# Last round of a mixture-of-experts tail: down weights by column halves, final scales spread by products, outputs on two queues

## The chip, the cores and the metric

One core of one Trainium2 chip runs the whole kernel in one launch. The metric is device time of one execution in microseconds (us), median of the runs shown.

## The reference, cut to what matters

Two transformer blocks over 256 rows of 1024 features, all in float32. The second block ends in a mixture of 32 experts and a last normalisation, and only this end is touched:

```
for e in range(32):
    hid = silu(xn @ w_gate[e]) * (xn @ w_up[e])          # 1024 -> 256
    out = out + (hid * cw[..., e:e+1]) @ w_down[e]       # 256 -> 1024, cw is 0 but for two experts a row
h = h + out
y = h * rsqrt(mean(h * h, axis=-1) + 1e-6) * final_norm_g      # 1024 scales, one a column
```

## The kernel before, in words

The experts are sorted by how many rows chose them, and only the chosen rows are gathered into places. Ten rounds follow (`NP` is 10). Rounds 0 to 3 take two experts with 64 places each, rounds 4 to 9 take four experts with 32 places each, so that 128 places fill the partitions in every round. A round `p` goes through these steps, each with a name in `moe`:

- `gu(p, 0)` and `gu(p, 1)` (line 1540) multiply the gathered rows by gate and up weights, half of the 1024 features at a time; `act(p)` (lines 1547 to 1549) makes the hidden values `hid`, 128 places by 256;
- `trans(p)` (line 1554) turns `hid` on TensorE, and ScalarE copies it out of PSUM as `hT` (line 1556);
- `dn(p)` (line 1562) multiplies `hT` by the down weights, 256 to 1024. The output is made in two halves of 512 columns, `c` 0 and 1; in each half two blocks of the 256 (`f` 0 and 1) are accumulated, and within each the experts follow one another. Each half is split into a rounded high part `y` on ScalarE (line 279) and the rest on VectorE (line 280);
- `scatter(p)` (line 1571) adds the places back to their rows: for each half of the columns and each half `t` of the rows, two products (high, then rest) into one of four accumulators `acc[t, c]` in PSUM.

The steps of neighbouring rounds are interleaved: `first(p)` holds `gu(p, 0)`; `down(p - 1)` holds `trans(p - 1)`, `scatter(p - 2)` for `c` 0, `dn(p - 1)`, and `scatter(p - 2)` for `c` 1; `second(p)` holds `gu(p, 1)` and `act(p)`. After the loop come `scatter(8)`, the load of the final scales, and `last`: `trans(9)`, `dn(9)` for both halves, `scatter(9)` for both halves. Then `write` normalises and sends out. This part of the kernel stands under a manual schedule: every engine, and every queue on which an engine issues transfers, runs its instructions in the order in which the program writes them.

Weights come through transfers that SyncE (SP) issues in the order of the list `self.raws`. A load (`Raw`) holds 1 MB, and there is room for 18 of them: 7 `big` and 3 `big2` buffers, and 16 small ones of which a load takes two. `_loads` hands out loads as long as a buffer is free, after each step. In round 9 the four experts' down weights take small buffers: each expert is fetched by two transfers of 512 KB, one for each `f`, with 4 KB of contiguous memory for each partition (line 1454). The final scales are one transfer from the same queue, whose source is repeated for all 128 partitions (line 1632).

`write` needs the sum of squares of each row. For each of the four accumulators ScalarE squares and sums (line 363); VectorE multiplies half 0 by its scales into `xgf` (line 1643), adds the two sums (line 1647), makes the mean (line 354), GpSimd raises it to the power -1/2 (line 356); then VectorE makes half 1 of the output (`o`, line 1652), ScalarE scales half 0 (line 1654), and SP issues four transfers of 256 KB to the output (lines 1653 and 1655).

Of the kernel before, what the change touches and what calls it, by code (L numbers as in the profile page):

```python
# [20 lines left out]
D = 1024  # L21
P = 128
# [77 lines left out]
class Net:  # L100
# [1317 lines left out]
    def moe(self):  # L1418
# [28 lines left out]
        def load_d(e):  # L1447
            def f(parts):
                rows = e.of(wd).rearrange("(p f) n -> p f n", f=2)
                if len(parts) == 1:  # L1450
                    nc.sync.dma_start(parts[0].rearrange("p (f c) n -> p f (c n)", f=2), rows)
                else:
                    for f in range(2):
                        nc.sync.dma_start(parts[f].rearrange("p c n -> p (c n)"), rows[:, f])
            return known(Raw(f, "d"), e)
        xs = self.xs
        def gu_of(raw, k):

            x = raw[k * len(raw) // 4].rearrange("p a b -> p (a b)").rearrange("p (j k n) -> p j k n", j=2, n=256)
            return x[:, :, k % (4 // len(raw)), :]  # L1460
        d_of = lambda raw, f, c: raw[0][:, 2 * f + c, :] if len(raw) == 1 else raw[f][:, c, :]
        oh, xg, stt, cwc, rsl = {}, {}, {}, {}, {}

        NP, NB = ROUNDS, BATCHES
# [92 lines left out]
        def dn(p, tiles, cols=range(2)):  # L1557
            for c in cols:
                q = self.pt()
                for f in range(2):  # L1560
                    for x, s in zip(tiles, own(p)):
                        nc.tensor.matmul(q[s], hT[p][:, f, s], d_of(x, f, c), start=f == 0, stop=f == 1)  # L1562
                h, l = self.act([P, 512], F32R, name="y"), self.act([P, 512], F32R, name="y")
                self.split(q, h, l)
                y[p, c] = (h, l)
# [13 lines left out]
                                     stop=False)  # L1579
        self.ids = None  # L1580
        gus = [[[load_gu(e, hf) for e in of_round(p)] for hf in range(2)] for p in range(NP)]
        ds = [[load_d(e) for e in of_round(p)] for p in range(NP)]
        for p in range(NP):
            if p:
                self.raws.extend(ds[p - 1])
            self.raws.extend(gus[p][0] + gus[p][1])
        self.raws.extend(ds[NP - 1])
        def first(p, tiles):
            gu(p, 0, tiles)
            b, j = divmod(p, 2)  # L1590
            if p == 0:
                gather(0, range(4, 8))
                slots_of(0)
                residual(1)
            if b < NB - 1 and j == 0:
                onehots(b + 1)
        def down(p, tiles):
            trans(p)
            if p:
                scatter(p - 1, [0])  # L1600
            dn(p, tiles)
            if p:
                scatter(p - 1, [1])
# [12 lines left out]
                self.rawpart(ds[p - 1], lambda *tiles, p=p: down(p - 1, tiles))  # L1616
            self.rawpart(gus[p][1], lambda *tiles, p=p: second(p, tiles))
        self.step(lambda: scatter(NP - 2))
        self.step(self.final_gain)
        def last(*tiles):  # L1620
            trans(NP - 1)
            for c in range(2):
                dn(NP - 1, tiles, [c])
            for c in range(2):
                scatter(NP - 1, [c])
        self.rawpart(ds[NP - 1], last)
        self.step(lambda: self.write([[acc[t, c] for c in range(2)] for t in range(2)]))

    def final_gain(self):

        self.gfin = self.act([P, D], name="gfin")
        self.nc.sync.dma_start(self.gfin, self.a["final_norm_g_2"][None, :].broadcast_to([P, D]))

    def write(self, x):

        nc, v, g = self.nc, self.nc.vector, self.gfin
        ss = [[self.small([P, 1]) for _ in range(2)] for _ in range(2)]
        xg = [self.act([P, 512], name="xgf") for _ in range(2)]
        for c in range(2):
            for t in range(2):  # L1640
                ss[t][c] = self.sumsq(x[t][c], 512)
                if c == 0:
                    v.tensor_tensor(xg[t], x[t][0], g[:, 0:512], op=ALU.mult)
        r = []
        for t in range(2):
            s = self.small([P, 1])
            v.tensor_tensor(s, ss[t][0], ss[t][1], op=ALU.add)
            r.append(self.power(s, D))
        for t in range(2):
            ts = slice(t * P, (t + 1) * P)  # L1650
            o = self.act([P, 512], name="o")
            v.scalar_tensor_tensor(o, x[t][1], r[t], g[:, 512:D], op0=ALU.mult, op1=ALU.mult)
            nc.sync.dma_start(self.out[0, ts, 512:D], o)
            nc.scalar.mul(xg[t], xg[t], r[t])
            nc.sync.dma_start(self.out[0, ts, 0:512], xg[t])

    def overflow(self):

# [2 lines left out]
        with self.tc.If(most >= 64 * 65):  # L1661
            left, m = self.act([P, 2 * E]), self.act([P, 2, 2, E])
            cap = self.act([P, E], name="cap")
            v.tensor_scalar(cap, self.key, self.order[:, WIDE - 1:WIDE], 32.0, op0=ALU.is_ge, op1=ALU.mult)
            v.tensor_scalar(cap, cap, 32.0 - 1000.0, None, op0=ALU.add)
            l3 = left.rearrange("p (t e) -> p t e", t=2)
            v.tensor_tensor(l3, self.pm, cap[:, None, :].to_broadcast([P, 2, E]), op=ALU.is_ge)
            v.tensor_tensor(m, self.sel2, self.w12[:, :, :, None].to_broadcast([P, 2, 2, E]), op=ALU.mult)
            for k in range(2):
                v.tensor_tensor(m[:, :, k, :], m[:, :, k, :], l3, op=ALU.mult)  # L1670
            v.tensor_tensor(l3, m[:, :, 0, :], m[:, :, 1, :], op=ALU.add)
            xT = [self.act([P, 4, S], name="xT") for _ in range(2)]
            for t in range(2):
                xn = self.act([P, D], name="xn")
                v.tensor_tensor(xn, *(x.bitcast(F32) for x in self.xs[t]), op=ALU.add)
                v.tensor_scalar(xn, xn, self.rf[:, t:t + 1], None, op0=ALU.mult)
                for i in range(2):
                    p = self.pt((P, 4, P))
                    for k in range(4):
                        kt = 4 * i + k  # L1680
                        nc.tensor.transpose(p[:, k, :], xn[:, kt * P:(kt + 1) * P], self.ident)
                        nc.scalar.mul(xT[i][:, k, t * P:(t + 1) * P], p[:, k, :], self.col("ffn_cols", kt, 1))
            self.X = [self.act([P, D], name="x") for _ in range(2)]
            for t in range(2):
                for c in range(2):
                    v.tensor_copy(self.X[t][:, c * 512:(c + 1) * 512], self.acc[t, c])
            for e in range(E):
                w = []
                for n in ("w_exp_gate_2", "w_exp_up_2"):
                    x = self.big([P, 8, 256], F32, "wo")  # L1690
                    for c in range(2):
                        rows = a[n][0, e, c * 512:(c + 1) * 512, :]
                        nc.sync.dma_start(x[:, 4 * c:4 * c + 4, :], rows.rearrange("(p k) n -> p k n", k=4))
                    w.append(x)
                wd = self.big([P, 2, D], F32, "wo")
                nc.sync.dma_start(wd, a["w_exp_down_2"][0, e].rearrange("(f p) n -> p f n", p=P))
                hid = self.act([P, 2, S], name="ho")
                for f in range(2):
                    q = []
                    for i in range(2):  # L1700
                        p = self.pt()[:, 0:S]
                        for k in range(8):
                            nc.tensor.matmul(p, w[i][:, k, f * P:(f + 1) * P], xT[k // 4][:, k % 4, :], start=k == 0,
                                             stop=k == 7)
                        q.append(p)
                    h = hid[:, f, :]
                    nc.scalar.activation(h, q[0], AF.Tanh, scale=0.5)
                    v.scalar_tensor_tensor(h, h, 1.0, q[0], op0=ALU.add, op1=ALU.mult)
                    v.tensor_tensor(h, h, q[1], op=ALU.mult)
                for t in range(2):  # L1710
                    for c in range(2):
                        p = self.pt()
                        for f in range(2):
                            nc.tensor.matmul(p, hid[:, f, t * P:(t + 1) * P], wd[:, f, c * 512:(c + 1) * 512],
                                             start=f == 0, stop=f == 1)
                        s = self.X[t][:, c * 512:(c + 1) * 512]
                        v.scalar_tensor_tensor(s, p, left[:, t * E + e:t * E + e + 1], s, op0=ALU.mult, op1=ALU.add)
            self.write([[x[:, 0:512], x[:, 512:D]] for x in self.X])


@with_exitstack
# [53 lines left out]
```

## Time and profile before

| what | value |
|---|---|
| median of 3 runs | 972.24 us (971.6 to 977.51) |
| profiled execution, its time | 971.25 us |
| profiled execution, its span | 969.5 us |
| busy share of the span: TensorE, VectorE, ScalarE, GpSimd | 93%, 56%, 49%, 4% |
| mean granted TensorE clock | 0.966 of full |

The span runs from the first to the last instruction of the program; the execution's own time is 1.75 us longer. The profiled execution lies 0.99 us under the median. In the rows below, PE is TensorE, PEld its weight loads, DVE is VectorE, ACT ScalarE, POOL GpSimd; SPq and ACTq are the queues on which SyncE and ScalarE issue transfers. Times are from the start of the span.

### The profile page before, as it was taken

Reading aid. Unit: us, or ns where it says so; the run is one execution under the profiler, and the core shown is the slowest. Engines: PE = TensorE matmul, PEld = TensorE weight load, DVE = VectorE, ACT = ScalarE, POOL = GpSimd, SP = SyncE. Lnnn points to the kernel's source line nnn. Section 1 sums busy time; section 2 is a strip of 40 time slices with the busy share of each in tenths; the row PEclk is TensorE's granted clock in tenths of the full one; section 3 lists DMA queues with packets and bytes.
Section 4 is the critical chain, followed back from the end, with each engine's and each line's share of the span. In section 5 each row is a group of like instructions: output and inputs, shape, how many; then the busy total and the mean of one; then the engine's idle time right before and its main releaser. Section 6 shows DMA issues by size and latency. Waiting matters only on the chain.

```text
span 969.5 us, 14260 instructions
## 1 busy us (share of the span) xinstructions
PE 900.0 (93%) x5265; PEld 697.7 (72%) x5265; DVE 547.4 (56%) x1101; ACT 472.6 (49%) x900; POOL 34.6 (4%) x71
## 2 busy tenths in 40 slices
PE   6999999999999999999999999999989999647775
PEld 5889898888999999988888887998864444213112
DVE  5986889776675555577765568755455221101002
ACT  5666789654664544456666635545432323002002
POOL 4200000000000000000200000000000000000000
PEclk9999999999999999999999999999998999779868
DMA  9644235495375555544854544454848999999994
GB/s 292 217 153 153 88 131 177 140 321 176 108 247 185 202 178 190 178 145 145 259 180 153 188 150 161 164 184 138 307 166 322 403 405 406 402 406 410 375 408 174
DMA packets 97784, 222.65 MB, mean 230 GB/s; under 512 B 9378, under 2 KB 13739, under 8 KB 96427
## 3 DMA queue, kind: packets, MB, share of 16 engines
q1 hardware_dynamic: 94016, 218.91, 63.5%
q10 hardware_dynamic: 3691, 2.74, 0.9%
q8 instruction: 44, 0.72, 0.3%
q14 instruction: 33, 0.27, 0.1%
HBM read 220.59 MB, written 1.05 MB: 229 GB/s over the span
## 4 chain that ended last, share of the span: by engine, by line
PE 80%; DMA 13%; DVE 3%; issue 1%; ACT 1%; POOL 0%; SPq 0%; DVEq 0%; ACTq 0%; POOLq 0%
PE acc L313 18%; PE acc L315 18%; PE acc L314 17%; DMA raw<-in_w_exp_up_dram 6%; PE pt L1540 5%; PE pt L314 3%; PE pt L315 3%; PE pt L313 3%; DMA rawa<-in_w_exp_down_dram 3%; PE pt L1562 2%; PE pt L1490 1%; DMA rawa<-in_w_exp_up_dram 1%; PE pt L286 1%; DMA raw<-in_w_exp_gate_dram 1%; PE acc L1571 1%
## 5 line engine op out<-in xcount | busy, mean ns | idle before, releaser
L280 DVE TENSOR_TENSOR w<-raw,w 128x512 fp32r<-128x512 f32 (+4 forms) x288 | 273.6, 969 | 115.6 <-ACT w L279 113.6
L279 ACT CAST w<-raw 128x512 fp32r<-128x512 f32 (+4 forms) x288 | 236.3, 847 | 153.9 <-PE acc L315 117.0
L313 PE MATMUL acc<-w,st 128*128 128x512 f32 (+2 forms) x508 | 197.2, 392 | 0.0
L314 PE MATMUL acc<-w,st 128*128 128x512 f32 (+2 forms) x508 | 196.9, 388 | 0.0
L315 PE MATMUL acc<-w,st 128*128 128x512 f32 (+2 forms) x508 | 192.9, 388 | 0.2 <-DVE w L280 0.2
L1540 PE MATMUL pt<-raw,xg 128*32 128x512 f32 (+1 forms) x360 | 95.7, 669 | 40.3 <-DMA raw<-in_w_exp_up_dram 40.3
L315 PEld LDWEIGHTS acc<-w,st 128*128 128x128 f32 x508 | 95.5, 188 | 18.9 <-DVE w L280 0.6
L313 PEld LDWEIGHTS acc<-w,st 128*128 128x128 f32 x508 | 95.8, 189 | 18.4 <-ACT st L279 0.5
L314 PEld LDWEIGHTS acc<-w,st 128*128 128x128 f32 x508 | 95.7, 189 | 17.4 <-DVE st L280 0.2
L1540 PEld LDWEIGHTS pt<-raw,xg 128*32 128x32 f32 (+1 forms) x360 | 22.1, 126 | 95.1 <-issue 91.4
L280 DVE TENSOR_TENSOR y<-pt,y 128x512 fp32r<-128x512 f32 x20 | 13.8, 692 | 129.3 <-ACT y L279 129.3
L314 PE MATMUL pt<-st,w 128*128 128x256 f32 x256 | 72.4, 283 | 1.9 <-DVE w L280 1.9
L315 PE MATMUL acc<-st,w 128*128 128x256 f32 x256 | 73.7, 288 | 0.0
L313 PE MATMUL acc<-st,w 128*128 128x256 f32 x256 | 73.5, 287 | 0.0
L314 PE MATMUL acc<-st,w 128*128 128x256 f32 x256 | 73.4, 287 | 0.0
L313 PE MATMUL pt<-st,w 128*128 128x256 f32 x256 | 72.3, 283 | 0.0
L315 PE MATMUL pt<-st,w 128*128 128x256 f32 x256 | 71.8, 283 | 0.0
L1556 ACT COPY hT<-pt 128x256 f32<-128x256 f32 x10 | 3.7, 373 | 97.4 <-PE pt L1554 97.4
L314 PEld LDWEIGHTS pt<-st,w 128*128 128x128 f32 x256 | 49.1, 192 | 2.3 <-DVE w L280 2.1
L313 PE MATMUL acc<-w,hid 128*128 128x512 f32 x128 | 50.0, 390 | 0.0
L314 PE MATMUL acc<-w,hid 128*128 128x512 f32 x128 | 49.9, 390 | 0.0
L315 PE MATMUL acc<-w,hid 128*128 128x512 f32 x128 | 49.8, 389 | 0.0
(393 smaller groups left out, 1391.0 us busy)
## 6 DMA issues: line engine op xcount, KB each, us to landing
raw<-in_w_in_dram SPq DMA_DIRECT2D x31, 1024.0 KB, 5.3
raw<-in_w_exp_gate_dram SPq DMA_DIRECT2D x45, 512.0 KB, 9.5
raw<-in_w_exp_up_dram SPq DMA_DIRECT2D x45, 512.0 KB, 10.2
rawa<-in_w_exp_down_dram SPq DMA_DIRECT2D x44, 512.0 KB, 9.1
raw<-in_w_up_dram SPq DMA_DIRECT2D x16, 1024.0 KB, 5.7
raw<-in_w_down_dram SPq DMA_DIRECT2D x16, 1024.0 KB, 6.2
raw<-in_w_exp_down_dram SPq DMA_DIRECT2D x10, 1024.0 KB, 11.0
rawa<-in_w_exp_gate_dram SPq DMA_DIRECT2D x38, 256.0 KB, 7.8
```

What stands on the lines that cost most here:

```text
L279: self.nc.scalar.copy(h, src)
L280: self.nc.vector.tensor_sub(l, src, h.bitcast(F32))
L286: self.nc.tensor.transpose(p[:, i, :], src[:, i * P:(i + 1) * P], self.ident)
L313: mm(acc, xh, wh, start=start, stop=False)
L314: mm(acc, xl, wh, start=False, stop=False)
L315: mm(acc, xh, wl, start=False, stop=stop)
L1490: nc.tensor.matmul(p, xs[t][i][:, k * P:(k + 1) * P], oh[b, t], start=n == 0, stop=n == 3)
L1540: nc.tensor.matmul(guP[p][q].rearrange("s (j f) -> s j f", j=2), xg[b, hf][:, k, j * P + q.start:j * P + q.stop], gu_of(x, k), start=kt == ...
L1556: nc.scalar.copy(hT[p], q)
L1562: nc.tensor.matmul(q[s], hT[p][:, f, s], d_of(x, f, c), start=f == 0, stop=f == 1)
L1571: nc.tensor.matmul(acc[t, c], stt[b][:, j, t, :], y[p, c][i], start=False, stop=p == NP - 1 and i == 1)
```

## The change

Three edits, all at the end.

1. The down weights of round 9 are loaded and used by halves of columns. A load now holds half `c` of the columns of two experts (`load_dc`), by two transfers of 512 KB, one for each expert; a partition's share of a transfer is two pieces of 2 KB. All of half 0 is asked for ahead of half 1. `last(c)` is called twice: for half 0 it does `trans(9)`, `final_gain`, `dn(9)` of half 0, `scatter(9)` of half 0, and the first part of `write`; for half 1 `dn`, `scatter`, and the rest of `write`.
2. The final scales come as one 4 KB transfer of 8 rows of 128, issued by ScalarE in `first(9)` (`load_gain`). `final_gain` spreads them to all partitions with eight products whose stationary operand is one column of the identity repeated 128 times, and two ScalarE copies out of PSUM.
3. `write` is cut in two: half 0's squares and scale products are written right behind half 0's `scatter`; the sum of both halves' squares is folded into the instruction that makes the mean. The two outputs `xgf` are issued by ScalarE instead of SP.

```diff
+        def load_dc(es, c):
+
+            def f(parts):
+                for i, e in enumerate(es):
+                    rows = e.of(wd).rearrange("(p f) n -> p f n", f=2)[:, :, c * 512:(c + 1) * 512]
+                    nc.sync.dma_start(parts[0][:, 2 * i:2 * i + 2, :] if len(parts) == 1 else parts[i], rows)
+            return known(Raw(f, "d"), es[1])
...
+        dc_of = lambda raw, i, f: raw[0][:, 2 * i + f, :] if len(raw) == 1 else raw[i][:, f, :]
...
                 for f in range(2):
-                    for x, s in zip(tiles, own(p)):
-                        nc.tensor.matmul(q[s], hT[p][:, f, s], d_of(x, f, c), start=f == 0, stop=f == 1)
+                    for i, s in enumerate(own(p)):
+                        w = d_of(tiles[i], f, c) if p < NP - 1 else dc_of(tiles[i // 2], i % 2, f)
+                        nc.tensor.matmul(q[s], hT[p][:, f, s], w, start=f == 0, stop=f == 1)
...
-        ds = [[load_d(e) for e in of_round(p)] for p in range(NP)]
+        ds = [[load_d(e) for e in of_round(p)] for p in range(NP - 1)]
+        tail = of_round(NP - 1)
+        ds_last = [[load_dc(tail[i:i + 2], c) for i in range(0, len(tail), 2)] for c in range(2)]
...
-        self.raws.extend(ds[NP - 1])
+        self.raws.extend(ds_last[0] + ds_last[1])
...
+            if p == NP - 1:
+                self.load_gain()
...
         self.step(lambda: scatter(NP - 2))
-        self.step(self.final_gain)
-        def last(*tiles):
-            trans(NP - 1)
-            for c in range(2):
-                dn(NP - 1, tiles, [c])
-            for c in range(2):
-                scatter(NP - 1, [c])
-        self.rawpart(ds[NP - 1], last)
-        self.step(lambda: self.write([[acc[t, c] for c in range(2)] for t in range(2)]))
+        def last(c, tiles):
+            if c == 0:
+                trans(NP - 1)
+                self.final_gain()
+            dn(NP - 1, tiles, [c])
+            scatter(NP - 1, [c])
+            self.write(c, [acc[t, c] for t in range(2)])
+        for c in range(2):
+            self.rawpart(ds_last[c], lambda *tiles, c=c: last(c, tiles))
+
+    def load_gain(self):
+
+        self.grow = self.act([P, P], name="grow")
+        self.nc.scalar.dma_start(self.grow[0:8, :], self.a["final_norm_g_2"].rearrange("(k n) -> k n", k=8))

     def final_gain(self):

         self.gfin = self.act([P, D], name="gfin")
-        self.nc.sync.dma_start(self.gfin, self.a["final_norm_g_2"][None, :].broadcast_to([P, D]))
-
-    def write(self, x):
+        for c in range(2):
+            p = self.pt((P, 4, P))
+            for i in range(4):
+                k = 4 * c + i
+                self.nc.tensor.matmul(p[:, i, :], self.ident[0:8, k:k + 1].to_broadcast([8, P]), self.grow[0:8, :],
+                                      start=True, stop=True)
+            self.nc.scalar.copy(self.gfin[:, c * 512:(c + 1) * 512], p.rearrange("q i n -> q (i n)"))
+
+    def write(self, c, x):

         nc, v, g = self.nc, self.nc.vector, self.gfin
...
+        if c == 0:
+            self.xgf, self.ms = [], []
             for t in range(2):
-                ss[t][c] = self.sumsq(x[t][c], 512)
-                if c == 0:
-                    v.tensor_tensor(xg[t], x[t][0], g[:, 0:512], op=ALU.mult)
+                ss = self.sumsq(x[t], 512)
+                xg, ms = self.act([P, 512], name="xgf"), self.small([P, 1])
+                v.tensor_tensor(xg, x[t], g[:, 0:512], op=ALU.mult)
+                v.tensor_scalar(ms, ss, 1.0 / D, EPS, op0=ALU.mult, op1=ALU.add)
+                self.xgf.append(xg)
+                self.ms.append(ms)
+            return
         r = []
         for t in range(2):
-            s = self.small([P, 1])
-            v.tensor_tensor(s, ss[t][0], ss[t][1], op=ALU.add)
-            r.append(self.power(s, D))
+            ss, ms, rt = self.sumsq(x[t], 512), self.small([P, 1]), self.small([P, 1])
+            v.tensor_scalar(ms, ss, 1.0 / D, self.ms[t], op0=ALU.mult, op1=ALU.add)
+            nc.gpsimd.tensor_tensor(rt, ms, self.mhalf[:, 0:1], op=ALU.pow)
+            r.append(rt)
         for t in range(2):
             ts = slice(t * P, (t + 1) * P)
             o = self.act([P, 512], name="o")
-            v.scalar_tensor_tensor(o, x[t][1], r[t], g[:, 512:D], op0=ALU.mult, op1=ALU.mult)
+            v.scalar_tensor_tensor(o, x[t], r[t], g[:, 512:D], op0=ALU.mult, op1=ALU.mult)
             nc.sync.dma_start(self.out[0, ts, 512:D], o)
-            nc.scalar.mul(xg[t], xg[t], r[t])
-            nc.sync.dma_start(self.out[0, ts, 0:512], xg[t])
+            nc.scalar.mul(self.xgf[t], self.xgf[t], r[t])
+            nc.scalar.dma_start(self.out[0, ts, 0:512], self.xgf[t])
```

## Rows read from the trace of the kernel before

**Rows 1.** The page: busy share of the 16 transfer engines in 40 equal slices.

```profile
DMA  9644235495375555544854544454848999999994
```

**Rows 2.** The chain that ended last, 930 to 970 us: start, length, what.

```profile
944.18 10.06 DMA rawa<-in_w_exp_down_dram
...
954.29 2.76 PE pt L1562 x18
...
959.76 0.12 DVE s L1647
...
960.20 0.55 POOL s L356
...
960.77 0.76 DVE o L1652
```

**Rows 3.** Timeline of PE, 938 to 957 us: start, length, instructions, idle before.

```profile
940.26 0.63 PE L1562 MATMUL pt<-rawa,hT 128*32 128x512 f32 x3
...
948.55 2.14 PE L1571 MATMUL acc<-y,sT 128*128 128x512 f32 x8
950.53 0.39 PE L1554 MATMUL pt<-ident,hid 128*128 128x128 f32 x2
951.38 1.06 PE L1562 MATMUL pt<-rawa,hT 128*32 128x512 f32 x6 [0.46 <-ACT hT L1556]
```

**Rows 4.** Timeline of ACT, 915 to 960 us.

```profile
915.34 0.47 ACT L1547 ACTIVATE th<-pt,s 128x256 f32<-128x256 f32 x1 [4.10 <-PE pt L1540]
939.44 0.37 ACT L1556 COPY hT<-pt 128x256 f32<-128x256 f32 x1 [23.63 <-PE pt L1554]
942.31 0.59 ACT L279 CAST y<-pt 128x512 fp32r<-128x512 f32 x1 [2.50 <-PE pt L1562]
...
958.99 0.60 ACT L363 ACTIVATE junk<-acc 128x512 f32<-128x512 f32 x1
```

**Rows 5.** Timeline of DVE, 942 to 959 us.

```profile
942.93 0.69 DVE L280 TENSOR_TENSOR y<-pt,y 128x512 fp32r<-128x512 f32 x1 [26.15 <-ACT y L279]
...
957.71 0.69 DVE L280 TENSOR_TENSOR y<-pt,y 128x512 fp32r<-128x512 f32 x1 [1.02 <-ACT y L279]
```

**Rows 6.** Timeline of the SP queue, 936 to 963 us: when transfers are issued.

```profile
936.26 0.33 SPq L1445 DMA_DIRECT2D rawa<-in_w_exp_up_dram  x1
...
942.83 1.69 SPq L1454 DMA_DIRECT2D rawa<-in_w_exp_down_dram  x3
945.43 0.34 SPq L1632 DMA_DIRECT2D gfin<-in_final_norm_g_dram  x1
...
961.55 0.35 SPq L1653 DMA_DIRECT2D out_dram<-o  x1
...
962.96 0.40 SPq L1655 DMA_DIRECT2D out_dram<-xgf  x1
```

**Rows 7.** Waits of the SP queue, 0 to 30 us: total, times, longest.

```profile
SPq L309 <- DMA free<-in_free_dram: 2.4, 1, 2.4
...
SPq L523 <- DMA rows<-in_rows_dram: 1.3, 1, 1.3
```

**Rows 8.** Stretches: length, busy (count) by engine, PE clock, DMA share, GB/s.

```profile
839.00:841.00 2.00, 2.00 (x15) 0.56 (x8) 0.00 (x0) 0.00 (x0) 0.00 (x0) 1.00 1.06 385
853.00:862.00 9.00, 0.00 (x0) 0.00 (x0) 0.67 (x2) 0.00 (x0) 0.00 (x0) 0.61 1.02 408
916.00:919.00 3.00, 0.00 (x0) 0.00 (x0) 0.75 (x2) 0.00 (x0) 0.00 (x0) 1.00 1.03 414
920.00:925.00 5.00, 0.00 (x0) 0.00 (x0) 0.00 (x0) 0.00 (x0) 0.00 (x0) 0.50 1.02 415
...
964.00:965.00 1.00, 0.00 (x0) 0.00 (x0) 0.00 (x0) 0.00 (x0) 0.00 (x0) 0.63 1.01 373
```

**Rows 9.** Line 647, two float32 products of 128 columns: durations, first and last start.

```profile
L647 PE MATMUL pt<-ident,rb x4: 270/274/275, 27.0 to 27.3; 128*128 128x128 f32 x4
```

**Rows 10.** Transfers that ScalarE issues: count, size, us to landing.

```profile
wr<-in_w_router_dram ACTq DMA_DIRECT2D x1, 144.0 KB, 9.5
```

More of the change, by code (lines that the diff above doesn't have):

```diff
@@ L1636, in write @@
+    def write(self, c, x):
         nc, v, g = self.nc, self.nc.vector, self.gfin
-        ss = [[self.small([P, 1]) for _ in range(2)] for _ in range(2)]
-        xg = [self.act([P, 512], name="xgf") for _ in range(2)]
-        for c in range(2):
+        if c == 0:
+            self.xgf, self.ms = [], []
             for t in range(2):
-                ss[t][c] = self.sumsq(x[t][c], 512)
-                if c == 0:
-                    v.tensor_tensor(xg[t], x[t][0], g[:, 0:512], op=ALU.mult)
+                ss = self.sumsq(x[t], 512)
[5 more added lines that the diff above has]
+            return
@@ L1717, in overflow @@
                         v.scalar_tensor_tensor(s, p, left[:, t * E + e:t * E + e + 1], s, op0=ALU.mult, op1=ALU.add)
-            self.write([[x[:, 0:512], x[:, 512:D]] for x in self.X])
+            for c in range(2):
+                self.write(c, [x[:, c * 512:(c + 1) * 512] for x in self.X])
 @with_exitstack
```

## The prediction, made before the changed kernel ran

> **What bounds the kernel now.** I read the page first, then the chain that ended last, then the timelines of the last 40 us engine by engine. From about 750 us on the transfer engines are at nine tenths or more [rows 1]: the last stage runs at the pace of the weights. But the change touches only its end, and there the question is which wait ends last. The chain says that the last down load was issued at 944.18, landed 10.06 us later, and that TensorE then had 2.76 us of products left, after which come scatter, squares, the power on GpSimd and the outputs [rows 2]. From this alone, halves of columns should pay: after the last landing only part of one half would be left instead of one f-block of half 0 and all of half 1.
>
> The PE timeline says something else [rows 3]. Until 950.92 TensorE is busy with `scatter(8)` and `trans(9)`, `hT` arrives at 951.38, and the first down product starts then. It stalls on data only from there to 954.29. So the weights are ahead of TensorE by only 2.9 us at the end, and whatever is put on TensorE or ScalarE before 951.38 moves the end.
>
> **The change part by part.**
>
> *Down weights by halves.* The bytes are the same, the pieces 2 KB instead of 4 KB. Where 256 KB loads with 2 KB pieces ran, the rate was 385 GB/s, against 408 where 4 KB pieces ran [rows 8]. So 4.19 MB take 10.9 instead of 10.3 us, and the stream ends 0.6 us later, at 954.9. Half 0 is then complete four transfers of 1.36 us earlier, at 949.5, before `hT`; half 1 at 954.9. Neither will be waited for, as the next sum shows.
>
> *The order on TensorE.* A half of `dn` has its cast on ScalarE 2.05 us after its first product starts (942.31 against 940.26 [rows 3, 4]) and its rest from VectorE 3.36 us after (942.93 + 0.69 [rows 5]). Before, half 1's products ran while half 0 was being split. Now `scatter(9)` of half 0 stands between the two, so TensorE waits there for VectorE. That cover is gone, and `dn` of half 1, queued behind it, waits too. A scatter product takes 0.27 us (2.14 for 8 [rows 3]); three of the four come after the rest is ready.
>
> *The scales.* Eight float32 products of 128 columns, put between `trans(9)` and `dn(9)`. Line 647 has two such products as four records that start 0.1 us apart and last 0.27 [rows 9]: sixteen records are 1.7 us. TensorE is free at 950.92, so they end at 952.6; 0.46 of them hides under the `hT` copy, 1.25 us is on the path. If a product took one record it would be 0.35 us; that is the lower end. The two ScalarE copies lie behind the `hT` copy and beside products, and cost nothing unless the cast of half 0 came before 954. The 512 KB transfer that goes away was issued behind all weights, at 945.43 [rows 6], and delayed nothing: no gain.
>
> *Sum of the tail.* Half 0 starts at 952.6; its rest is ready at 955.96; three scatter products, 956.8; half 1 starts there (its data landed at 954.9), its rest is ready at 960.15. Before, that was 957.71 + 0.69 = 958.40 [rows 5]: 1.75 later. From there ScalarE is free at once, where before the square began 0.59 us behind the rest (958.99 [rows 4]): 0.15 back, as the product itself needs some 0.45. One small sum of 0.12 to 0.19 us falls away between the square and GpSimd [rows 2]. The first output would start 1.45 us later.
>
> *Outputs on two queues.* SP issues the four at 961.55 to 962.96 [rows 6], 1.41 us from first to last, while the 1.05 MB take 2.8 us at the 373 GB/s of that stretch [rows 8]. The data, not the issue, ends last; from the rows, two queues can give 0 to 0.4 us. The Trainium skill, DMA: Bandwidth & Descriptors, section "Issuing engines are not separate DMA queues", says that transfers from any issuing engine run on the same 16 engines and that a second one saves only issuing time; by it the gain is 0 and the tail costs 1.45, by the 0.4 end of the rows 1.05. I take +1.2 for the tail, between -0.3 (products short, both output gains, stall shorter) and +1.8.
>
> *The new transfer on ScalarE's queue.* This is the largest term. It is a 4 KB load, so its bytes cost nothing, and it is wanted only after `trans(9)`. But it has to be issued, by ScalarE, in order. In this kernel a transfer waits until the one eight places before it has landed: the last down load is issued at 944.18, when the one issued at 936.26 has landed [rows 2, 6]. The count runs over both queues: at the start SP waits 2.4 us for `free` and 1.3 us for `rows`, which ScalarE had issued and whose data SP's loads don't need [rows 7]. So ScalarE will wait for some weight load, and behind that wait on ScalarE stands the `hT` copy of round 8, at 939.44 [rows 4]; behind it `dn(8)`, `gu(9, 1)`, and all of the tail.
>
> Which load? In ScalarE's order the new transfer comes right behind the activation of round 8 at 915.34 [rows 4]. There is room for 18 loads; 16 are taken when round 8's second half is used, so the last two of the four down loads (four transfers) get their buffers only from those very products. The row load should therefore be counted among these four or behind them, and the load eight before it is one whose landing lets SP issue one of the last transfers: 942.2 to 944.2, or 945.43 if it is counted last [rows 6]. I take 942.8 as the value, nearest to the place right behind the activation; with 0.35 us to issue, the `hT` copy starts at 943.2 instead of 939.44: +3.7 us, between 0 (counted earlier, or known to have landed) and 6.3. The load itself then has until 954.6 to land; the slowest that ScalarE issued took 9.5 us for 144 KB [rows 10].
>
> *The clock.* TensorE then idles from about 940.3 to 944.0. After a stop at 915.24 the granted clock was still full at 916 to 919 and half, 1.2 GHz, from 920 to 925 [rows 8]. A stop of 3.7 us may just be enough, and then the first 1 to 3 us of `dn(8)` run at half: +0 to 1.6, I take 0.5.
>
> The sum is 1.2 + 3.7 + 0.5 = +5.4 us against the profiled execution's own 971.25, or 976.65; that lies 0.99 below the median, so I predict 977.5.
>
> **The rivals.**
>
> 1. *No wait on ScalarE.* The transfer is counted before the last loads, or its place's forerunner has landed by 915.8. For it: loads issued before 905 have landed by then. Against it: [rows 7], and the order of buffers. Then only the tail counts: 972.24 + 1.2 = 973.4.
> 2. *The halves pay.* If the data, not TensorE, were what half 1 waits for, and ScalarE did not wait, then 1.7 us of half 0's and half 1's products leave the path behind the last landing, the later stream gives 0.6 back: 971.2. Against it stands the start of `dn(9)` at 951.38 [rows 3], which no part of the change brings forward.
> 3. *Slower, past the bound.* One mechanism: the row load is counted behind all eight down transfers. ScalarE then stands until the first of them has landed, at 945.43, `hT` comes 6.3 us late, and by then TensorE has idled 5.8 us, over the point at which the clock fell after 915.24, so that up to 2 us are lost at half clock. 972.24 + 1.2 + 6.3 + 2 = 981.7. It decides by one place in the order of transfers.
> 4. *The change does not do what it says:* the halves cannot overlap since `scatter(9)` of half 0 blocks TensorE. That is already in the forecast's tail; if the stall were shorter than worked out (rest in 2.5 us), the forecast drops by 0.9 to 976.6.
>
> **How the numbers follow.** Forecast (with rival 4's variant) 0.60; no wait 0.21; halves pay 0.07; past the bound 0.09; something else 0.03. The likeliest gives 977.5, with its own range 974.5 to 980.5. The range reaches down over the case without a wait and up to the third rival: 972.0 to 981.5. One per cent is 9.7 us, about what a measurement of this kernel can tell from no change; its three runs spread over 5.9. Faster by more than that has no mechanism here, 0.01; slower, part of the third rival, 0.07; within, 0.92.
>
> **What would show it.** Right: on ScalarE, a gap between the activation of round 8 and a transfer issue at 942 to 944, the `hT` copy behind it, TensorE idle for some 3 to 4 us before `dn(8)`, and the whole end moved by as much. In the tail, 1.7 us of products on the identity before `dn(9)`, then a gap of about 1.3 us between the two halves of `dn(9)`, no wait for a down load of half 1, and the first output 1.2 to 1.5 us later against `trans(9)`. Wrong: the new transfer issued at about 916, or products of half 1 waiting for their weights. The forecast fails most easily on the place of the row load in the order of transfers, which no row of before shows.

## The result, and the profile after

The changed kernel takes 979.03 us (median of 16 runs, 977.48 to 982.54) against 972.17 for the kernel before (16 runs beside it); the ratio is 1.0069, with a 95% interval of 1.0057 to 1.0081. That is 6.9 us slower, within one per cent, 1.5 us above the forecast and inside its range.

The profiled execution of after took 980.84 us, 1.8 above its median, with a span of 979.1. It was already late before the change could act: `trans(8)`, the last step ahead of the first new wait, starts 2.99 us later than in the profile of before. Experiment 5 below has that step later still (943.34) and is no slower than before, so I take this as a difference between executions and read times from that step on. First the timeline of ScalarE (start, length, instruction, idle before and what ended it), which answers to [rows 4]:

```profile
920.15 0.47 ACT L1555 ACTIVATE th<-pt,s 128x256 f32<-128x256 f32 x1 [4.08 <-PE pt L1548]
946.03 0.30 ACTq L1645 DMA_DIRECT2D grow<-in_final_norm_g_dram  x1
946.37 0.37 ACT L1564 COPY hT<-pt 128x256 f32<-128x256 f32 x1 [25.75 <-DMA rawa<-in_w_exp_up_dram]
```

Between the activation of round 8 and the `hT` copy stands the new transfer, and the copy's idle time is put down to a weight load, which a copy out of PSUM does not need. The chain that ended last says which load it was: one issued at 936.95 that took 9.06 us.

```profile
936.95 9.06 DMA rawa<-in_w_exp_up_dram
...
946.03 0.30 ACTq L1645
...
946.37 0.38 ACT hT L1564
...
946.79 5.18 PE pt L1571 x32
```

SP's queue has two more weight loads behind this one, and then the eight down transfers (line 1461), which SP issues between 940.79 and 949.4 as room in the count lets it:

```profile
936.95 0.33 SPq L1445 DMA_DIRECT2D rawa<-in_w_exp_up_dram  x1
938.23 0.33 SPq L1445 DMA_DIRECT2D rawa<-in_w_exp_gate_dram  x1
939.51 0.33 SPq L1445 DMA_DIRECT2D rawa<-in_w_exp_up_dram  x1
940.79 8.60 SPq L1461 DMA_DIRECT2D rawa<-in_w_exp_down_dram  x8
```

Now TensorE, which answers to [rows 3]; the line numbers of after are 8 to 9 higher.

```profile
941.89 0.50 PE L1562 MATMUL pt<-ident,hid 128*128 128x128 f32 x2
942.15 1.17 PE L1580 MATMUL acc<-y,sT 128*128 128x512 f32 x4
946.79 1.07 PE L1571 MATMUL pt<-rawa,hT 128*32 128x512 f32 x3 [3.47 <-ACT hT L1564]
...
950.08 0.60 PE L1571 MATMUL pt<-rawa,hT 128*32 128x512 f32 x3
...
953.03 0.63 PE L1548 MATMUL pt<-raw,xg 128*32 128x512 f32 x3
...
958.56 0.39 PE L1562 MATMUL pt<-ident,hid 128*128 128x128 f32 x2
958.88 2.05 PE L1654 MATMUL pt<-grow,ident 8*128 8x128 f32 x16
960.86 1.92 PE L1571 MATMUL pt<-rawa,hT 128*32 128x512 f32 x16
963.49 0.50 PE L1580 MATMUL acc<-y,sT 128*128 128x512 f32 x1 [0.71 <-ACT y L279]
964.22 0.98 PE L1580 MATMUL acc<-y,sT 128*128 128x512 f32 x3 [0.22 <-DVE y L280]
```

Two of the steps that this is measured against have no row above. In before's own timeline of TensorE they are:

```profile
938.90 0.51 PE L1554 MATMUL pt<-ident,hid 128*128 128x128 f32 x2
...
944.98 0.63 PE L1540 MATMUL pt<-raw,xg 128*32 128x512 f32 x3
```

The windows of after (length, busy time and count of PE, PEld, DVE, ACT and POOL, granted clock, transfer share, GB/s) show what the stop did to the clock: still full while TensorE waited, half in the first 3 us of `dn(8)`, and full again from 950. Half is the 1.2 GHz level, and three products that lasted 0.60 at full clock last 1.07.

```profile
943.50:946.50 3.00, 0.00 (x0) 0.00 (x0) 0.00 (x0) 0.13 (x1) 0.00 (x0) 1.00 1.04 385
946.80:949.80 3.00, 3.00 (x16) 0.78 (x20) 0.00 (x0) 0.00 (x0) 0.00 (x0) 0.50 1.05 386
950.00:952.00 2.00, 2.00 (x21) 0.47 (x13) 0.69 (x1) 0.59 (x1) 0.00 (x0) 1.00 1.05 387
```

From these rows, [rows 2, 3] and the two spans, the difference step by step (the row of 970.67, the first output, stands below the table):

| from | to | before | after | difference |
|---|---|---|---|---|
| start | `trans(8)` | 938.90 | 941.89 | +2.99 |
| `trans(8)` | `dn(8)` | 1.36 | 4.90 | +3.54 |
| `dn(8)` | `gu(9, 1)` | 4.72 | 6.24 | +1.52 |
| `gu(9, 1)` | `trans(9)` | 5.55 | 5.53 | -0.02 |
| `trans(9)` | `dn(9)` | 0.85 | 2.30 | +1.45 |
| `dn(9)` | first output being made | 9.39 | 9.81 | +0.42 |
| first output | end of span | 8.73 | 8.43 | -0.30 |

Without the first line, in which nothing of the change has run, this is +6.6 us, close to the 6.9 of the medians. Five of them (3.54 and 1.52) lie ahead of `trans(9)`, where all that the change adds is the issue of a 4 KB load. The end of after's chain, and VectorE's rest of half 1 in its timeline:

```profile
968.48 0.51 PE acc L1580
...
969.01 0.48 ACT junk L363
...
970.67 0.73 ACT xgf L1682
```

```profile
967.73 0.69 DVE L280 TENSOR_TENSOR y<-pt,y 128x512 fp32r<-128x512 f32 x1 [0.84 <-ACT y L279]
```

### The profile page after: what moved, and what is told of

Read it like the earlier page. It is cut to its first block, busy times and chain, and to the rows that moved or that the text cites. A ratio compares the mean times of both kernels' runs of the same rounds, so it can differ in the third digit from the quotient of the medians.

```text
span 979.1 us, 14296 instructions
## 1 busy us (share of the span) xinstructions
PE 907.2 (93%) x5281; PEld 702.1 (72%) x5281; DVE 547.7 (56%) x1101; ACT 473.4 (48%) x902; POOL 34.6 (4%) x71
## 4 chain that ended last, share of the span: by engine, by line
PE 80%; DMA 13%; DVE 3%; ACT 2%; issue 1%; SPq 0%; POOL 0%; ACTq 0%; POOLq 0%
PE acc L315 17%; PE acc L313 17%; PE acc L314 17%; PE pt L1548 5%; DMA raw<-in_w_exp_up_dram 3%; PE pt L314 3%; PE pt L315 3%; PE pt L313 3%; PE pt L1571 3%; DMA rawa<-in_w_exp_up_dram 2%; DMA raw<-in_w_exp_gate_dram 2%; DMA raw<-in_w_exp_down_dram 2%; DMA rawa<-in_w_exp_down_dram 2%; PE pt L286 1%; PE acc L1580 1%
## 5 line engine op out<-in xcount | busy, mean ns | idle before, releaser
L314 PEld LDWEIGHTS pt<-st,w 128*128 128x128 f32 x256 | 49.9, 195 | 2.4 <-DVE w L280 2.1
L313 PE MATMUL acc<-w,hid 128*128 128x512 f32 x128 | 50.0, 390 | 0.0
L313 PEld LDWEIGHTS pt<-st,w 128*128 128x128 f32 x256 | 49.8, 195 | 0.2
L314 PE MATMUL acc<-w,hid 128*128 128x512 f32 x128 | 49.9, 390 | 0.0
```

The source lines that it names most:

```text
L313: mm(acc, xh, wh, start=start, stop=False)
L314: mm(acc, xl, wh, start=False, stop=False)
```

## The experiments

My theory was the forecast's: most of the loss is ScalarE waiting to issue a 4 KB load, with a half clock behind it; the smaller part is the tail (products of the scales, the gap between halves). The rival was that the tail, or the loads by halves, cost most, and that the wait on ScalarE lies beside waits for weights anyway. Kernels 1 to 4 ran on one chip beside 30 runs of the kernel before (median 971.76), kernels 5 to 7 on another beside 27 (971.36).

**1. The row load moved out of the last stage.** In the profile it is issued at 150.52 us instead of 946.03, some 795 us earlier and not the 670 of the expectation. The tile is one that is dead by then, so that no memory is added.

```diff
         # in the setup, right behind the router's load
+        self.load_gain()
...
-            if p == NP - 1:
-                self.load_gain()
...
-        self.grow = self.act([P, P], name="grow")
+        self.grow = self.mask_band.rearrange("p a b -> p (a b)").bitcast(F32)
```

> The changed kernel with one thing moved: the 4 KB row of scales is loaded some 670 us earlier, next to the router's weights, into a buffer that is dead by then (the mask of block 1). Theory A, the load's place in the order of transfers makes ScalarE wait: the wait (3.5 us by the start of dn(8)) and the half clock behind it (1.5 us) go, the tail's 1.9 us stay, so 979.0 - 5.0 = 974.0 us. Theory B, the wait lies beside work that the weights hold up anyway and the loss is in the new tail: 978 to 979 us.

Measured: 974.33 (12 runs), ratio 1.0030 [1.0016, 1.0043]. By the two ratios some 4 us of the 6.9 are gone by moving one load. The timeline of ScalarE has the `hT` copy where it was in [rows 4], behind TensorE and nothing else, and TensorE's has the scale products still in the path:

```profile
939.43 0.37 ACT L1565 COPY hT<-pt 128x256 f32<-128x256 f32 x1 [23.39 <-PE pt L1563]
```

```profile
950.51 0.39 PE L1563 MATMUL pt<-ident,hid 128*128 128x128 f32 x2
950.83 2.05 PE L1653 MATMUL pt<-mask_band,ident 8*128 8x128 f32 x16
952.80 1.92 PE L1572 MATMUL pt<-rawa,hT 128*32 128x512 f32 x16
```

This trace has no shift against before (`trans(9)` at 950.51 against 950.53), so the tail stands alone: the first output is made at 962.60 instead of 960.77, 1.83 later.

**2. The row load alone.** The kernel before, with only the new load added at the same place; nothing reads it.

```diff
             if b < NB - 1 and j == 0:
                 onehots(b + 1)
+            if p == NP - 1:
+                self.load_gain()
```

> The kernel before with one thing added: the same 4 KB load issued by ScalarE in first(9), read by nothing; weights, scales and outputs as before. Theory A: ScalarE waits for the landing of the load eight places before, dn(8) starts 3.5 us late and runs partly at half clock, 972.2 + 5.0 = 977.2 us. Theory B: a load that nobody reads costs nothing, 972.2 us.

Measured: 975.93 (12 runs), ratio 1.0038 [1.0025, 1.0052]: one 4 KB load that nothing needs costs about 4 us. That is about 1 us less than the 5.0 expected. On TensorE `dn(8)` starts 5.04 late (945.30 against 940.26 [rows 3]; 0.26 of it is there before the wait, `trans(8)` at 939.16) and at half clock: `gu(9, 1)` follows 7.36 behind it, where it was 4.72. `dn(9)` starts 7.67 late (959.05 against 951.38), but then runs without a stop:

```profile
945.30 1.07 PE L1562 MATMUL pt<-rawa,hT 128*32 128x512 f32 x3 [4.71 <-ACT hT L1556]
...
952.66 0.63 PE L1540 MATMUL pt<-raw,xg 128*32 128x512 f32 x3
...
959.05 3.64 PE L1562 MATMUL pt<-rawa,hT 128*32 128x512 f32 x32 [0.46 <-ACT hT L1556]
```

Before, the last landing ended `dn(9)` at 957.05 (954.29 + 2.76 [rows 2]), 5.67 us after its start; here it takes 3.64. So 2 us of the lateness were swallowed, as `dn(9)` of the kernel before was held up by late weights anyway; for this part the rival was right.

**3. The scales as before.** The changed kernel with the old transfer on SP in place of row load and products; halves, the cut `write` and two output queues stay.

```diff
-            if p == NP - 1:
-                self.load_gain()
...
+        self.step(self.final_gain)          # ahead of last
...
-                self.final_gain()           # in last
...
-        for c in range(2):
-            p = self.pt((P, 4, P))
-            ...
+        self.nc.sync.dma_start(self.gfin, self.a["final_norm_g_2"][None, :].broadcast_to([P, D]))
```

> The changed kernel with the scales as before: one repeated transfer on SP behind the weights, no row load on ScalarE's queue and no products; halves of columns, the order of scatter, the split write and two output queues stay. Theory A: only the order of the two halves is left, 0.4 us by the traces, so 972.6 us (972.0 to 973.4). Theory B, the halves and the stall between them carry the loss: 977 us or more.

Measured: 972.36 (12 runs), ratio 1.0000 [0.9989, 1.0011]. To within that interval, 1 us either way, all of the loss belongs to the second edit, the spread of the scales. The halves and the two queues together are neither gain nor loss that these runs can tell.

**4. The gap filled.** The changed kernel with eight products of 256 columns on the identity in front of `dn(8)`, into a PSUM tile that nothing reads, so that TensorE works while ScalarE waits.

```diff
+            if p == NP - 2:
+                fill = self.pt()
+                for i in range(4):
+                    for f in range(2):
+                        k = 2 * i + f
+                        nc.tensor.matmul(fill[:, 0:S], self.ident, xg[p // 2, k // 4][:, k % 4, :], start=True, stop=True)
```

> The changed kernel with eight products of 256 columns on the identity put where TensorE idles before dn(8), 3.4 us of work into an unread PSUM tile. Theory A with the clock as a term of its own: the wait stays, the half clock in dn(8) goes, 979.0 - 1.5 = 977.5 us, and dn(8) shows 3.6 us again. Rival: the clock costs nothing as later steps wait for weights anyway, 979.0 us; should the filling outlast the wait, 979.5 us.

Measured: 977.49 (7 runs), ratio 1.0062 [1.0041, 1.0083]. On TensorE the filler lies in the wait, and `dn(8)` behind it runs at full clock: `gu(9, 1)` follows after 4.70 us, as before (4.72), where after has 6.24. The window is of the same kernel:

```profile
942.61 3.61 PE L1619 MATMUL pt<-xg,ident 128*128 128x256 f32 x16
946.15 0.63 PE L1571 MATMUL pt<-rawa,hT 128*32 128x512 f32 x3
...
950.85 0.63 PE L1548 MATMUL pt<-raw,xg 128*32 128x512 f32 x3
```

```profile
946.20:949.70 3.50, 3.50 (x33) 0.89 (x32) 0.69 (x1) 0.58 (x1) 0.00 (x0) 1.00 1.05 387
```

That the stop caused the half clock is thereby shown. What the clock costs in the median is not: the interval contains after's 1.0069, and the filler itself outlasted the `hT` copy (945.27 + 0.37) by half a us.

**5. All the waits taken out of the order.** Row load early as in 1 (issued at 151.58); products of the scales at the head of `first(9)`, where TensorE waits for weights; and in `last` both halves of `dn(9)` ahead of both scatters, as before the change.

```diff
+            if p == NP - 1:
+                self.final_gain()           # at the head of first
...
             dn(NP - 1, tiles, [c])
-            scatter(NP - 1, [c])
-            self.write(c, [acc[t, c] for t in range(2)])
+            if c == 0:
+                return
+            for c in range(2):
+                scatter(NP - 1, [c])
+                self.write(c, [acc[t, c] for t in range(2)])
```

> A version meant to keep what the halves can give: the row of scales loaded early as in the run before, its eight products at the start of first(9), where TensorE waits for weights, and both halves of dn(9) ahead of both scatters; half 0's squares still ahead of half 1's, outputs on two queues. Theory A: no wait on ScalarE, no products and no stall between trans(9) and the end; the last down load lands at 954.9 by the trace of the early row, half 1's rest is ready some 0.3 us before that of the kernel before, the first output starts 0.5 us earlier: 971.3 us, a ratio of 0.9995 that cannot be told from 1. Rival, the later landing of 2 KB pieces decides and the halves lose by themselves: 972.5 us or more.

Measured: 971.18 (11 runs), ratio 0.9996 [0.9987, 1.0005].

**6. As 5, with all outputs on SP's queue.**

```diff
-            nc.scalar.dma_start(self.out[0, ts, 0:512], self.xgf[t])
+            nc.sync.dma_start(self.out[0, ts, 0:512], self.xgf[t])
```

> The same with all four outputs on SP's queue. Theory A (the output's data, not its issue, ends last): 0 to 0.4 us over the two queues, 971.3 to 971.7 us. Rival, issue decides: 1 us more.

Measured: 970.46 (12 runs), ratio 0.9991 [0.9982, 1.0001]. One queue is not slower than two; their intervals overlap. The profile shows what the halves do once nothing else is in the way: here half 1 waits 0.26 us for its last load and has ten products left, where before 18 were left [rows 2].

```profile
952.26 3.08 PE L1572 MATMUL pt<-rawa,hT 128*32 128x512 f32 x22 [0.46 <-ACT hT L1565]
955.60 1.90 PE L1572 MATMUL pt<-rawa,hT 128*32 128x512 f32 x10 [0.26 <-DMA rawa<-in_w_exp_down_dram]
```

This is the fastest version I have, and it is not told from the kernel before.

**7. The row load one round earlier.** The changed kernel with the same load, on the same queue, issued in `first(8)`.

```diff
-            if p == NP - 1:
+            if p == NP - 2:
                 self.load_gain()
```

> The changed kernel with the row load issued one round earlier, in first(8). Theory A in its full form: ScalarE waits there too, and the copy of hT of round 7 behind it comes some us late, but after that round TensorE has some 10 us without weights, so the wait is swallowed and only the tail's 1.9 us remain: 974.0 us, as with the early row. Rival, a wait on ScalarE costs its length wherever it stands: 978 to 980 us.

Measured: 973.6 (10 runs), ratio 1.0026 [1.0015, 1.0037], the same as experiment 1. But the wait has not gone. The load is again issued when a weight load has landed, with the `hT` copy of round 7 behind it, and the activation of round 8 comes 8.17 us later than in [rows 4]:

```profile
912.98 0.30 ACTq L1645 DMA_DIRECT2D grow<-in_final_norm_g_dram  x1
913.32 0.37 ACT L1564 COPY hT<-pt 128x256 f32<-128x256 f32 x1 [23.27 <-DMA rawa<-in_w_exp_down_dram]
...
923.51 0.47 ACT L1555 ACTIVATE th<-pt,s 128x256 f32<-128x256 f32 x1 [4.09 <-PE pt L1548]
938.97 0.37 ACT L1564 COPY hT<-pt 128x256 f32<-128x256 f32 x1 [14.98 <-PE pt L1562]
```

TensorE stood for 6.76 us in round 7, longer than the 3.47 of after, and started again with products of 1.06, as long as those at half clock. Then it came to weights that were not there yet, and by `trans(8)` the whole lateness is gone (938.43 against 938.90). Before, it stood 10.20 us for the first of these weights (the last line below, from before's timeline); here 1.10, and 1.45 for the next.

```profile
913.74 1.06 PE L1571 MATMUL pt<-rawa,hT 128*32 128x512 f32 x1 [6.76 <-ACT hT L1564]
...
924.52 1.02 PE L1548 MATMUL pt<-raw,xg 128*32 128x512 f32 x2 [1.10 <-DMA raw<-in_w_exp_up_dram]
927.00 1.92 PE L1548 MATMUL pt<-raw,xg 128*32 128x512 f32 x2 [1.45 <-DMA raw<-in_w_exp_up_dram]
...
938.43 0.50 PE L1562 MATMUL pt<-ident,hid 128*128 128x128 f32 x2
```

```profile
925.45 1.89 PE L1540 MATMUL pt<-raw,xg 128*32 128x512 f32 x2 [10.20 <-DMA raw<-in_w_exp_up_dram]
```

## Why the prediction was right, and where its sizes were off

The terms miss by -0.16 (the wait, 3.54 against 3.7), +1.02 (the clock, 1.52 against 0.5) and +0.37 (the tail with the outputs, 1.87 - 0.30 against 1.2). So the total did not come out right by errors that cancel. The sum itself, 972.24 + 5.4, is 977.64; it was put down as 977.5.

**The wait on ScalarE: right, in place and size.** The forecast took the issue at 942.8 from [rows 6]. After's 946.03 less the 2.99 of shift is 943.04. The load that it waited for is the eighth before it, if five of the eight down transfers are counted ahead of it (five, and the loads of 939.51, 938.23 and 936.95). Then the next down transfer should wait for the load of 938.23, the one after for 939.51, and the last for the first down transfer, issued at 940.79. SP's queue in after has the last three at

```profile
946.80 0.54 SPq L1461 DMA_DIRECT2D rawa<-in_w_exp_down_dram  x1
947.58 0.54 SPq L1461 DMA_DIRECT2D rawa<-in_w_exp_down_dram  x1
948.84 0.54 SPq L1461 DMA_DIRECT2D rawa<-in_w_exp_down_dram  x1
```

and the transfers' own view, from windows that hold one issue each (size, us to landing), says that the load of 938.23 took 8.5 and the first down transfer 7.9, so that they landed at 946.7 and 948.7:

```profile
rawa<-in_w_exp_gate_dram SPq DMA_DIRECT2D x1, 256.0 KB, 8.5
...
rawa<-in_w_exp_down_dram SPq DMA_DIRECT2D x1, 512.0 KB, 7.9
```

So the new transfer is counted among the last four down transfers, as the forecast had it. In experiments 2 and 4 it is issued at 944.54 and 944.93, which is 944.28 and 942.50 less the shift of their `trans(8)` (939.16 and 941.33): the wait ends with a landing, and that moved by 1.8 us between these three traces. The `hT` copy came 3.94 later than it would have (4.48 behind `trans(8)` instead of 0.54), forecast 3.7. On TensorE 3.54 are left, since `scatter(7)` had kept `dn(8)` from starting at once in the kernel before; this cover of 0.40 I had not taken off. That the place in the count is the cause rests on these landings and on experiments 1, 2 and 7, in which the stall goes, comes and moves with the load's place.

**The clock: right in kind, too small.** The term was +0.5 with a bound of 1.6; the trace has +1.52. The step that failed is "may just be enough": I put the value near the lower end because the only row of a fall, in [rows 8], came later after its stop. The stop here, 3.47 us, sufficed. With this the forecast would have been 978.5. The bound was too low as well: behind the stop of 4.71 in experiment 2 the same step took 2.64 us more than before.

**The tail: right in its pieces, a little too small.** Forecast +1.2 with the gain of two queues, +1.45 up to the first output; measured +1.87 up to there. The products cost 1.45, not 1.25: sixteen records took 2.05 us, not 1.7. From the first product of `dn(9)` to the rest of half 1 it took 7.56 instead of 7.02 (967.73 + 0.69 - 960.86 against 958.40 - 951.38 [rows 3, 5]), +0.54 where I had 0.50. And 0.12 came back between that rest and the output, not 0.27 to 0.34: the square began 0.59 behind the rest as before (969.01 - 968.42), so the 0.15 that a free ScalarE was to give was not there. Half 1 never waited for its weights, and in experiment 1 the last down load landed at 954.9, as worked out from 385 GB/s; after moved 385 to 387 in the windows above. Experiments 1 and 3 differ by 2.0 us in their medians and only by the products and the place of the scales' load, which the 1.45 on the path fits within their intervals.

**The outputs.** From the start of the first output to the end of the span after has 0.30 less than before. But the same stretch is 8.34 in experiment 6 with one queue (961.16 to 969.5) and 8.43 in after with two, and experiment 6 is no slower than experiment 5: I count it as no gain. The rule of the Trainium skill that the forecast weighed (DMA: Bandwidth & Descriptors, "Issuing engines are not separate DMA queues"), that a second issuing engine saves only issuing time, agrees with 0.9991 against 0.9996: it bought nothing here. In experiment 6's profile the last output is issued at 963.37 and the span ends at 969.5, so the data ended last and not the issue.

**The rivals.** "No wait" fell with the 25.75 us of idle time at the `hT` copy; it would have been 973.4, and experiment 1, which makes it true, took 974.3. "The halves pay" needed half 1 to wait for data; only in experiment 6's profile does it, by 0.26, and there 0.9 us in the median is all that could be theirs, within the interval. The third rival had the count three places too far, behind eight down transfers instead of five. One reading at the start of the forecast was too strong: that whatever is put ahead of 951.38 moves the end. In experiment 2 the kernel before swallowed 2 us there; in the changed kernel half 1 waits for no weights, and nothing was swallowed.

**What stays open.** The clock's 1.5 us is read from traces (1.52 in after, none in experiment 4 with the stop filled) and was not separated by times. Why experiment 2 lost only 4 us is explained by its trace, not by a further run. Why a transfer waits for the eighth before it, no run here shows, and issuing the load from another queue than ScalarE's was not tried.

## What to carry to other kernels

A load's bytes can be free while its place is not: ask what the issuing engine must wait for before it can issue, and what stands behind that instruction on the same engine. Put small loads well ahead of the crowded stretch, as in experiment 1, or in a round whose engine waits for data anyway: issued in `first(9)` the load cost some 4 us, issued in `first(8)` no more than when it came early, though TensorE stood longer there. Before cutting the last operands into finer pieces, look at whether the consumer or the data comes last at the point of the cut.

## What the runs showed of the hardware

The eight down transfers with 2 KB pieces occupied SP's queue for 543 ns each (median), those with 4 KB pieces in before 333. Experiment 3, which has the 2 KB pieces, is at 1.0000, so no cost of this shows in the times. The lines are the ones of the two weight loads in a view by source line (ns least, median, most; first and last start), after, then before:

```profile
L1461 SPq DMA_DIRECT2D rawa<-in_w_exp_down_dram x8: 543/543/661, 940.8 to 948.8; - x8
```

```profile
L1454 SPq DMA_DIRECT2D rawa<-in_w_exp_down_dram x44: 328/333/948, 685.5 to 944.2; - x44
```

The granted clock was still 1.00 in the 3 us in which TensorE stood before 946.5, and 0.50 in the first 3 us of work behind them. Here the price of the stop was paid after it had ended.
